# Summing the rotated state's two parts before the output products, and making four low-part weight tiles by accumulating transfers

## The chip, the cores and the metric

The kernel runs on one core of one Trainium2 chip. The metric is the device time of one execution in microseconds. Three runs of the kernel before are shown, and one further execution was profiled.

## What is computed

Two residual layers on a 256 x 1024 sequence, all in float32. The first mixes with a diagonal complex state-space model (S5) and a gated unit, the second with causal attention over one block of 256 keys. Cut to the part that the change touches:

```python
proj = h @ w_in; u, z = proj[..., :1024], proj[..., 1024:]
bu = einsum(u, b)                       # per group of 16 channels, 64 complex states
s_re, s_im = associative_scan(a, f * bu)
y = einsum(s_re, c_re) - einsum(s_im, c_im) + d_skip * u
y = gelu(y)
y = y * sigmoid(y @ w_glu + b_glu)      # the gated unit
y = y * silu(z)
h = h + y @ w_out
```

## The kernel before

**Who sets the order.** The body does not issue instructions: it records operations in a list (`Program.add`), each with a cost in ns that a formula gives, its dependencies and a push (a bonus in priority). `Program.order` lays them out with these costs in a list schedule, forth and back several times, and `emit` then issues them in the order of the planned starts. Each engine runs its own queue strictly in that order. So a changed cost, one operation more or a moved call changes the order on all five engines.

**Tiles.** The 64 groups of channels stand as four blocks b = 0 to 3. `x_table`, `x_turn`, `k_table`, `y_table` and `w_table` (L847 and above) build small matrices from the model's parameters. `u_step` (k = 0 to 7) makes u from x and eight 512 KB weight tiles, with the transposes `x_turn8` and `b_turn` in between, and behind them `c_turn` (L694): 16 transposes of c into a PSUM tile `wide`, which ScalarE copies to the tile `yT`. `u_turn` then scales u (by `rum`, which VectorE copies from PSUM as tile `s`), sends it through the transfers `zz<-zz` and transposes it into `U`. `z_pair` (m = 0 to 3) are 64 products of 128 x 256 for the gate z, whose operands are ready early. Each leaves two records in the trace, as all float32 products do (transposes leave one).

**States.** For each block, `ssm_in` (32 products of 64 x 64) brings u into the states, `rotate` turns them by cosines and sines (`EC`, `ES`, made by `rotations`) and scans them along time, and `states` (L886) turns the result back. That result has two parts, `pa` (tile `tb`) and `pc` (tile `t`): the state is their sum. It is never formed. `ssm_within` writes the block's own 16 products into PSUM, and `ssm_out` (L926) adds 32 products with `pa` and then 32 with `pc`, with the same other operand `Y`; PSUM does the sum. ScalarE copies the block out (`ys`), TensorE transposes it, ScalarE applies gelu into `yT` and a rounding copy into `ah`, and VectorE makes the low part `al`.

**Weights in two parts.** From weight tile 16 on, each 128 x 1024 tile w (loaded into `wr`, four buffers) becomes a high part (`X` or `zh`: a rounding copy on ScalarE) and a low part (`xp` or `zl`: w minus high on VectorE), in `split_part` (L474). Even tiles use `X` and `xp`, odd ones `zh` and `zl`. `mm3` makes three products of them. Tiles 16 to 23 belong to the gated unit (`glu_tile`, 24 products each, 192 in all), tiles 24 to 31 to the output product behind it.

```python
        act(hi, raw[i][:, c0:c1])
        tt(V, lo, raw[i][:, c0:c1], hi.bitcast(F), SUB)
```

All operations are issued in `emit`, so the trace has them all at L355, and tiles tell them apart.

Of the kernel before, what the change touches and what calls it, by code (L numbers as in the profile page):

```python
# [20 lines left out]
F = mybir.dt.float32  # L21
# [54 lines left out]
class Program:  # L76
# [67 lines left out]
    def add(self, handle, eng, method, a, k):  # L144
# [9 lines left out]
        if dma:  # L154
            cost = self.ISSUE[eng]
        elif eng == "PE":
            if method == "transpose":
                cost = 109 if aps[0].shape[0] >= 64 else 30
            else:
                m, c = n(aps[0]), n(aps[1])  # L160
                if aps[0].dtype == FR:
                    cost = 4 + 0.4455 * max(c, 256)
                else:
                    cost = max(4 * c / 2.4 + 2, 109) * m / 128 * aps[0].shape[0] / 128
                    if m == 32:
                        cost = 42
        elif eng == "DVE":
            two = method in ("tensor_tensor", "scalar_tensor_tensor", "tensor_tensor_scan", "tensor_reduce") or psum
            cost = (70 if not psum else 125) + n(aps[0] if method == "tensor_reduce" else out) * (6.4 if method == "reciprocal" else 2.1 if method == "tensor_tensor_scan" else 1.04 if two else 0.53)
        elif eng == "ACT":  # L170
            cost = 95 + 0.83 * n(aps[0]) + (60 if len(aps) > 1 else 0) + (100 if "accum_out" in k else 0)
        else:
            spread = any(not x.ap[-1][0] for x in aps)
            each = {"memset": 0.85, "tensor_scalar": 5.2}.get(method, 1.8 if spread else 2.2)
            cost = 150 + 205 * n(out) if k.get("op") == OP.pow else 60 + n(out) * each
# [25 lines left out]
        if eng == "ACT" and not dma:  # L201
            f = a[2] if len(a) > 2 else AF.Copy
            op.table = {AF.Silu: 0, AF.Sin: 0, AF.Gelu_apprx_tanh: 1, AF.Exp: 2}.get(f)
        if dma:
            run = out.ap[-1][1] if len(aps[0].ap) > 1 else 1
            run = min(aps[0].ap[-1][1], out.ap[-1][1]) if aps[0].ap[-1][0] == 1 else 1
            op.nbytes = int(np.prod(out.shape)) * 4 * (1 if run * 4 >= 512 else 2)
        for x, w in [(x, False) for x in aps] + [(x, True) for x in outs]:
# [19 lines left out]
                    keep.append(e)  # L228
            keep.append((op.i, w, p0, p1, bits))
            self.seen[name] = keep  # L230
    grouping, chain, only, behind, push = False, None, None, None, 0

    @contextmanager
    def fixed(self, only=None):
# [121 lines left out]


RATE = 270
MODE = 3000
TICK, BUSY = 10240 / 3, 3600  # L360
SAME = {"PE": 0, "DVE": 127, "ACT": 140, "POOL": 95, "SP": 0}
# [23 lines left out]
def body(ctx: ExitStack, tc: tile.TileContext, x, norm_g, w_in1, a_re, a_im, log_dt, b_re, b_im,  # L385
# [88 lines left out]
    def split_part(i, c0, c1):  # L474
        if i not in whl:
            load_to(i + 1)
            own = i % 2
            whl[i] = (tile_([128, 1024], FR, name="zh" if own else "X", bufs=NZ if own else NX),
                      tile_([128, 1024], FR, name="zl" if own else "xp", bufs=NZ if own else NP_))
        hi, lo = (w[:, c0:c1] for w in whl[i])  # L480
        act(hi, raw[i][:, c0:c1])
        tt(V, lo, raw[i][:, c0:c1], hi.bitcast(F), SUB)

    def split_to(n):
        while state["split"] < min(n, len(plan)):
# [96 lines left out]
    vec = tile_([128, 24], F, name="vec")  # L582
    PE.transpose(pt[:, 256:272], vn, ident[:16, :16])
    V.tensor_copy(vec[:, 0:16], pt[:, 256:272])
    xT = tile_([128, 8, S], F, name="ah")

    def x_turn8(k):
# [228 lines left out]
    def k_table(b):  # L816

        p = wide()
        xv = X[b].rearrange("p (r q x) -> p r q x", r=2, q=8)
        with prog.group():  # L820
            for r in range(2):
                for a in range(2):
                    for hh in range(4):
                        for j2 in range(2):
                            o = 512 * j2 + 16 * hh
                            PE.matmul(p[side(a), o:o + 16], xv[side(j2), r, 2 * hh + a], ct_[side(j2), r, 8 * b + 2 * hh + a],
                                      start=(r == 0 and hh == 0), stop=(r == 1), skip_group_check=True)
        kv = lambda t: t[:, 8 * b:8 * b + 8].rearrange("p (h j) c -> p h j c", j=2)
        tt(V, kv(KS), p.rearrange("p (j x) -> p j x", j=2)[:, :, 0:64].rearrange("p j (h c) -> p h j c", c=16), kv(dm), ADD)

# [16 lines left out]
    def ssm_in(b):  # L847

        p = wide()
        prog.push = 10000  # L850
        with prog.group():
            for ri in range(2):
                for hh in range(4):
                    for j2 in range(2):
                        for a in range(2):
                            o = 512 * a + (4 * ri + hh) * 64
                            PE.matmul(p[side(j2), o:o + 64], XT[b][side(a), 4 * ri + hh, side(j2)],
                                      U[side(a), 4 * b + hh, side(j2)], start=True, stop=True)
        prog.push = 0
        vts[b] = p  # L860

    PSTS = {}
# [23 lines left out]
    def states(b, t2, p):  # L886

        ec, es = (t[:, :, :M - 1] for t in turns[b])
        pa, pc = tmp("tb", NT), tmp("t3", NQ)
        gm = lambda t: t.rearrange("p (r g m) -> p r g m", r=2, m=M)  # L890
        first = lambda t: t.rearrange("p (g m) -> p g m", m=M)[:, :, 0]
        G.memset(first(pc), 0.0)
        ts(V, first(pa), p[1][:, 0:16], 0.0, 0.0, MIN, MAX)
        z = gm(t2)[:, :, :, :M - 1]
        tt(V, gm(pa)[:, :, :, 1:], z, bc(ec[:, None], [128, 2, 8, M - 1]), MUL)
        stt(V, gm(pc)[:, 0, :, 1:], z[:, 1], -1.0, es, MUL, MUL)
        tt(V, gm(pc)[:, 1, :, 1:], z[:, 0], es, MUL)
# [12 lines left out]
    def ssm_within(b):  # L910

        if b % 2:
            p = wide().rearrange("p (j x) -> p j x", j=2)
            p = p[:, 0], p[:, 1]
        else:
            p = acc(), acc()
        prog.push = 20000
        with prog.group():
            for h in range(4):
                for j2 in range(2):  # L920
                    for a in range(2):
                        product(p, h, a, j2, U[side(a), 4 * b + h, side(j2)], W[side(a), 8 * b + 2 * h + j2], h == 0, False)
        prog.push = 0
        return p

    def ssm_out(b, p):  # L926
        for i, t in enumerate(PSTS[b]):
            tv = t.rearrange("p (r a h m) -> p r a h m", r=2, a=2, h=4)
            with prog.group():
                for r in range(2):  # L930
                    for h in range(4):
                        for a in range(2):
                            for j2 in range(2):
# [29 lines left out]
    with prog.fixed("PE"):  # L963
        for k in range(8):
# [2 lines left out]
                x_turn8(n)  # L967
            if k == 1:
                b_turn()
    load_to(14)  # L970
    prog.push = 10000
    c_turn()
    prog.push = 0
    pv0 = wide()
    PE.transpose(pv0[:, 0:8], vb, ident[32:40, 32:40])
    V.tensor_copy(vec[:, 16:24], pv0[:, 0:8])
    for i in range(2):
        PE.matmul(pv0[:, 8:10], cst[:, C_RU + 128 * i:C_RU + 128 * i + 128], rse[:, i], start=(i == 0), stop=(i == 1))
    rum = small([128, 2])
# [342 lines left out]
```

## Time and profile before

| | us |
|---|---|
| three runs | 296.65, 296.05, 292.43 (median 296.05) |
| the profiled execution: its time | 293.73 |
| its span in the trace | 291.9 |
| outside the span | 1.8 |

The span is cut as follows: to 28 us loads, parameters and the first half of u; to 53 us the rest of u and the tables; to 109 us gate, states and their products; to 134 us the gated unit; then the output product, and from 150 us on attention. Times of rows are us from the span's start; TensorE has an engine for products (PE) and one for loading their weights (PEld).

### The profile page before, as it was taken

How to read it: one execution, taken by the hardware profiler on the slowest of the kernel's cores; microseconds unless marked ns; L12 is line 12 of the kernel's file. 1: busy time of each engine (PE TensorE's matmuls, PEld its weight loads, DVE VectorE, ACT ScalarE, POOL GpSimd, SP SyncE). 2: the span in 40 equal slices, each digit the busy share in tenths (PEclk: the TensorE clock that was granted, in tenths of full speed). 3: DMA queues.
4: the chain of work that ended last, by engine and by line, in shares of the span. 5: the costliest groups of instructions: out<-in, count | busy, mean ns of one | idle time of the engine just before them, and what ended most of it. 6: DMA issues, size and time to landing. Idle time of an engine off the chain costs nothing.

```text
span 291.9 us, 6324 instructions
## 1 busy us (share of the span) xinstructions
PE 280.2 (96%) x2551; PEld 229.0 (78%) x2551; DVE 214.9 (74%) x430; ACT 159.1 (55%) x306; POOL 22.7 (8%) x26
## 2 busy tenths in 40 slices
PE   8998999999998969999999999899999999999995
PEld 7454458888677859998888888678888799998884
DVE  0959789998958647976439648898679988699603
ACT  2579347377440358766429347557565766585300
POOL 3100013000000000000000014500013100000000
PEclk9999999999999988999999999999999999999999
DMA  5999454882000193876745643565245472434003
GB/s 177 244 331 277 126 161 122 213 227 76 0 2 2 39 271 131 240 216 207 212 137 153 209 149 138 165 201 187 96 138 162 136 214 77 144 120 166 6 0 144
DMA packets 41596, 43.91 MB, mean 150 GB/s; under 512 B 4552, under 2 KB 31136, under 8 KB 41504
## 3 DMA queue, kind: packets, MB, share of 16 engines
q1 hardware_dynamic: 40608, 42.68, 50.2%
q10 hardware_dynamic: 864, 0.82, 0.8%
q8 instruction: 20, 0.33, 0.5%
q14 instruction: 8, 0.07, 0.1%
q0 software_dynamic: 96, 0.02, 0.0%
HBM read 41.41 MB, written 1.05 MB: 145 GB/s over the span
## 4 chain that ended last, share of the span: by engine, by line
PE 73%; DVE 7%; DMA 6%; ACT 5%; issue 4%; POOL 3%; SPq 1%; ACTq 0%; POOLq 0%
PE uz L355 33%; PE acc L355 23%; PE wide L355 17%; DMA zz<-in_x_dram 4%; POOL sm L355 3%; DVE sm L355 2%; DMA wr<-in_attn_w_in_dram 2%; DVE D L355 2%; ACT ES L355 1%; SPq L355 1%; DVE xp L355 1%; DVE zl L355 1%; ACT EC L355 1%; DVE X L355 1%; ACT X L355 1%
## 5 line engine op out<-in xcount | busy, mean ns | idle before, releaser
L355 DVE TENSOR_TENSOR xp<-wr,X 128x1024 fp32r<-128x1024 f32 x28 | 34.0, 1222 | 13.8 <-ACT X L355 13.7
L355 DVE TENSOR_TENSOR zl<-wr,zh 128x1024 fp32r<-128x1024 f32 x28 | 34.1, 1219 | 6.6 <-ACT zh L355 6.5
L355 ACT ACTIVATE zh<-wr 128x1024 fp32r<-128x1024 f32 x28 | 29.4, 1056 | 15.7 <-PE uz L355 7.9
L355 ACT ACTIVATE X<-wr 128x1024 fp32r<-128x1024 f32 x28 | 29.5, 1057 | 14.7 <-PE uz L355 8.1
L355 PE MATMUL uz<-al,zh 128*128 128x256 f32 x96 | 24.5, 349 | 0.0
L355 PEld LDWEIGHTS uz<-al,zh 128*128 128x128 f32 x96 | 17.9, 190 | 2.7 <-issue 0.8
L355 POOL TENSOR_TENSOR sm<-sm,mhalf 128x4 f32<-128x4 f32 x8 | 13.7, 1714 | 50.7 <-DVE sm L355 50.6
L355 PE MATMUL uz<-zh,ah 128*128 128x512 f32 x40 | 17.6, 490 | 0.0
L355 PE MATMUL acc<-zh,ah 128*128 128x512 f32 x40 | 17.6, 484 | 0.0
L355 PE MATMUL uz<-zl,ah 128*128 128x512 f32 x40 | 17.1, 478 | 0.0
L355 PE MATMUL acc<-zl,ah 128*128 128x512 f32 x40 | 17.1, 476 | 0.0
L355 PE MATMUL uz<-al,zl 128*128 128x256 f32 x64 | 16.6, 389 | 0.0
L355 PEld LDWEIGHTS uz<-al,zl 128*128 128x128 f32 x64 | 11.4, 190 | 3.0 <-issue 1.6
L355 DVE TENSOR_TENSOR Y<-acc,Y 128x512 f32<-128x512 f32 x4 | 2.8, 691 | 11.4 <-PE acc L355 11.4
L355 PEld LDWEIGHTS acc<-zl,ah 128*128 128x128 f32 x40 | 7.5, 189 | 4.2 <-issue 3.3
L355 DVE TENSOR_TENSOR tb<-s,yT 128x512 f32<-128x512 f32 x16 | 10.7, 682 | 0.0
L355 ACT ACTIVATE ys<-acc 128x256 f32<-128x256 f32 (+1 forms) x8 | 3.8, 496 | 12.4 <-PE acc L355 12.3
L355 PEld LDWEIGHTS acc<-zh,ah 128*128 128x128 f32 x40 | 7.4, 190 | 3.9 <-issue 2.9
L355 PEld LDWEIGHTS uz<-zl,ah 128*128 128x128 f32 x40 | 7.3, 189 | 3.3 <-issue 2.2
L355 PEld LDWEIGHTS uz<-zh,ah 128*128 128x128 f32 x40 | 7.3, 189 | 3.3 <-issue 2.4
L355 PE MATMUL uz<-X,ah 128*128 128x512 f32 x24 | 9.9, 411 | 0.0
L355 PE MATMUL acc<-X,ah 128*128 128x512 f32 x24 | 9.8, 408 | 0.0
(279 smaller groups left out, 804.8 us busy)
## 6 DMA issues: line engine op xcount, KB each, us to landing
wr<-in_attn_w_in_dram SPq DMA_DIRECT2D x32, 512.0 KB, 4.2
zl<-in_ssm_w_in_dram SPq DMA_DIRECT2D x8, 512.0 KB, 6.8
wr<-in_ssm_w_glu_dram SPq DMA_DIRECT2D x8, 512.0 KB, 6.3
wr<-in_ssm_w_out_dram SPq DMA_DIRECT2D x8, 512.0 KB, 4.3
wr<-in_attn_w_out_dram SPq DMA_DIRECT2D x8, 512.0 KB, 4.3
zh<-in_ssm_w_in_dram SPq DMA_DIRECT2D x7, 512.0 KB, 8.4
zz<-zz SPq DMA_DIRECT2D x8, 128.0 KB, 2.3
Y<-in_x_dram SPq DMA_DIRECT2D x2, 512.0 KB, 5.2
```

The lines of the kernel that those rows point to most:

```text
L355: getattr(handle, method)(*map(self.real, a), **{q: self.real(v) for q, v in k.items()})
```

## The change

Five things are changed. (1) `SUM`: for all four blocks VectorE adds `pc` to `pa`, and `ssm_out` makes one set of 32 products instead of two. (2) `LOW_DMA`: for tiles 16 to 19 the low part isn't made on VectorE. ScalarE copies the negative high part into it, and GpSimd issues a transfer that adds the weight tile from DRAM on top (2 MB are thus read a second time). (3) `CT`: `c_turn` stands behind `u_step(5)` in the fixed order of TensorE, and not after `u_step(7)` with a push. (4) The transpose of `b_glu` and its copy into `vec` go to the start. (5) The planner's costs of small products are set one by one (`unit`).

```diff
-                    if m == 32:
-                        cost = 42
+                    if self.unit:
+                        cost = self.unit
...
+        if dma and "accum_op" in k:
+            op.nbytes = int(np.prod(out.shape)) * 8
...
+EARLY = {}
+CT = 5
+LOW_DMA = (16, 17, 18, 19)
+SUM = (0, 1, 2, 3)
...
         act(hi, raw[i][:, c0:c1])
-        tt(V, lo, raw[i][:, c0:c1], hi.bitcast(F), SUB)
+        if i in LOW_DMA:
+            act(lo, hi.bitcast(F), AF.Copy, scale=-1.0)
+            G.dma_start(lo.rearrange("p (k n) -> p k n", k=8), plan[i], accum_op=ADD)
+        else:
+            tt(V, lo, raw[i][:, c0:c1], hi.bitcast(F), SUB)
...
+    PE.transpose(pt[:, 272:280], vb, ident[32:40, 32:40])
+    V.tensor_copy(vec[:, 16:24], pt[:, 272:280])
...
         tt(V, gm(pc)[:, 1, :, 1:], z[:, 0], es, MUL)
+        if b in SUM:
+            tt(V, pa, pa, pc, ADD)
+            pc = None
         PSTS[b] = pa, pc
...
-        for i, t in enumerate(PSTS[b]):
-            tv = t.rearrange("p (r a h m) -> p r a h m", r=2, a=2, h=4)
+        parts_ = [t.rearrange("p (r a h m) -> p r a h m", r=2, a=2, h=4) for t in PSTS[b] if t is not None]
+        prog.unit = 31
+        for tv in parts_:
...
             if k == 1:
                 b_turn()
+            if k == CT:
+                c_turn()
...
-    prog.push = 10000
-    c_turn()
-    prog.push = 0
+    if CT > 7:
+        prog.push = 10000
+        c_turn()
+        prog.push = 0
     pv0 = wide()
-    PE.transpose(pv0[:, 0:8], vb, ident[32:40, 32:40])
-    V.tensor_copy(vec[:, 16:24], pv0[:, 0:8])
```

The three places below are all on ScalarE. In the names, the last number tells tiles of one name apart, the one before it the buffer.

The first place is before the scaling of u. `yT<-wide` is the copy of c, `EC` and `ES` are the cosines and sines of a block (1 or 2), `zz<-uz` is the scaled u. Before:

```order
L355 ACTIVATE ah_0_127<-wide_1_322,vec_0_120 128x256
L355 ACTIVATE ah_0_127<-wide_0_328,vec_0_120 128x256
L355 ACTIVATE D0_1_316<-D0_1_316 128x8
L355 ACTIVATE yT_0_267<-wide_1_341 128x512 x2
L355 ACTIVATE EC_2_378<-ES_2_259 128x512
L355 ACTIVATE EC_2_378<-EC_2_378,s13_0_93 128x512
L355 ACTIVATE ES_2_259<-ES_2_259 128x512
L355 ACTIVATE rrow_0_397<-wide_1_388 128x256
L355 ACTIVATE zz_0_410<-uz_0_138,s15_0_406 128x512
```

After:

```order
L357 ACTIVATE EC_1_357<-ES_1_201 128x512
L357 ACTIVATE EC_2_363<-ES_2_256 128x512
L357 ACTIVATE EC_1_357<-EC_1_357,s13_0_93 128x512
L357 ACTIVATE EC_2_363<-EC_2_363,s13_0_93 128x512
L357 ACTIVATE ES_1_201<-ES_1_201 128x512
L357 ACTIVATE yT_0_271<-wide_1_359 128x512 x2
L357 ACTIVATE ES_2_256<-ES_2_256 128x512
L357 ACTIVATE rrow_0_405<-wide_1_397 128x256
L357 ACTIVATE zz_0_414<-uz_0_137,s15_0_409 128x512
```

Block 1's three operations, which stood further up, now stand ahead of the copy of c, with two of block 2.

The second place is the second half of u. `um` is what comes back from the transfers, `U2<-acc` are the transposed tiles that `ssm_in` of blocks 2 and 3 reads, `X`, `xp` and `zh` belong to weight tiles 16 to 18. Before:

```order
L355 ACTIVATE um_0_639<-zz_0_410 128x8x64 x2
L355 ACTIVATE X_2_661<-wr_0_623 128x1024
L355 ACTIVATE zh_2_674<-wr_1_627 128x1024
L355 ACTIVATE U2_0_520<-acc_0_668 128x512
L355 ACTIVATE U2_0_520<-acc_1_671 128x512
```

After:

```order
L357 ACTIVATE um_0_604<-zz_0_414 128x8x64 x2
L357 ACTIVATE X_2_684<-wr_0_572 128x1024
L357 ACTIVATE xp_0_690<-X_2_684 128x1024
L357 ACTIVATE X_0_701<-wr_2_583 128x1024
L357 ACTIVATE U2_0_563<-acc_0_695 128x512
L357 ACTIVATE U2_0_563<-acc_1_697 128x512
```

Between `um` and `U2` stand three whole-tile copies instead of two: the high and the negative copy of tile 16, and the high part of tile 18.

The third place is the end of the states. `ys` are blocks copied out, `zz<-uz` the last two gate pairs, then gelu into `yT`. Before:

```order
L355 ACTIVATE ys_0_1117<-acc_0_966 128x16x16
L355 ACTIVATE ys_0_1117<-acc_1_969 128x16x16
L355 ACTIVATE ys_1_1176<-wide_0_984 128x16x16 x2
L355 ACTIVATE zz_0_793<-uz_0_913 128x2x4x64
L355 ACTIVATE zz_0_793<-uz_1_922 128x2x4x64
L355 ACT_TABLE_LOAD
L355 ACTIVATE yT_0_1284<-uz_0_1244 128x4x64
L355 ACTIVATE ys_0_1356<-acc_0_1156 128x16x16
L355 ACTIVATE ys_0_1356<-acc_1_1159 128x16x16
L355 ACTIVATE yT_0_1284<-uz_0_1244 128x4x64
```

After:

```order
L357 ACTIVATE ys_0_1111<-acc_0_982 128x16x16
L357 ACTIVATE ys_0_1111<-acc_1_985 128x16x16
L357 ACTIVATE ys_1_1117<-wide_0_1003 128x16x16 x2
L357 ACTIVATE zz_0_931<-uz_0_941 128x2x4x64
L357 ACTIVATE zl_0_1169<-zh_0_979 128x1024
L357 ACTIVATE zz_0_931<-uz_1_949 128x2x4x64
L357 ACT_TABLE_LOAD
L357 ACTIVATE yT_0_1216<-uz_0_1175 128x4x64 x2
L357 ACTIVATE ys_0_1267<-acc_0_1120 128x16x16
L357 ACTIVATE ys_0_1267<-acc_1_1123 128x16x16
```

The negative copy of tile 19 (`zl`) now stands between the last two gate pairs.

## Rows read from the trace of the kernel before

**Rows 1.** Page, part 1: busy time, share of the span and instructions.

```profile
PE 280.2 (96%) x2551; PEld 229.0 (78%) x2551; DVE 214.9 (74%) x430; ACT 159.1 (55%) x306; POOL 22.7 (8%) x26
```

**Rows 2.** Windows: us busy (instructions) of PE, PEld, DVE, ACT, POOL; clock, DMA share, GB/s.

```profile
108.00:112.00 4.00, 4.00 (x22) 3.66 (x21) 0.36 (x2) 3.17 (x9) 0.00 (x0) 0.62 0.88 296
112.00:133.00 21.00, 21.00 (x179) 21.00 (x178) 17.51 (x33) 14.66 (x28) 0.00 (x0) 1.00 0.63 185
```

**Rows 3.** Timeline, TensorE, first and last product of the gated unit.

```profile
109.30 0.56 PE L355 MATMUL wide<-ah,zh 128*128 128x256 f32 x1
...
133.54 0.28 PE L355 MATMUL wide<-ah,zl 128*128 128x256 f32 x1
```

**Rows 4.** Timeline, TensorE, 92 to 108 us (start, us, engine, operation, count [idle before]).

```profile
92.32 1.11 PE L355 MATMUL wide<-Y,tb 64*64 64x64 f32 x64
93.26 0.39 PE L355 MATMUL wide<-Y,t 64*64 64x64 f32 x11
94.59 0.98 PE L355 MATMUL wide<-Y,t 64*64 64x64 f32 x51 [0.94 <-issue]
...
99.56 1.56 PE L355 MATMUL uz<-al,zl 128*128 128x256 f32 x6
...
103.41 1.10 PE L355 MATMUL wide<-Y,t 64*64 64x64 f32 x61
107.42 0.33 PE L355 MATMUL wide<-Y,t 64*64 64x64 f32 x3 [2.92 <-issue]
```

**Rows 5.** Timeline, ScalarE, 101 to 115 us.

```profile
101.16 1.15 ACT L355 ACTIVATE zz<-uz 128x512 f32<-128x512 f32 x1 [2.39 <-PE uz L355]
102.33 1.28 ACT L355 ACT_TABLE_LOAD   x1
...
108.83 1.54 ACT L355 ACTIVATE yT<-uz 128x256 f32<-128x256 f32 x3 [3.05 <-PE uz L355]
110.17 0.69 ACT L355 ACTIVATE ys<-wide 128x256 f32<-128x256 f32 x2
110.75 0.64 ACT L355 ACTIVATE yT<-uz 128x256 f32<-128x256 f32 x1
...
114.51 0.43 ACT L355 ACTIVATE ah<-yT 128x256 fp32r<-128x256 f32 x1
```

**Rows 6.** Timeline, TensorE, 28 to 48 us.

```profile
28.15 1.21 PE L355 MATMUL wide<-cst,Y 64*128 64x64 f32 x16 [1.00 <-ACT ah L355]
...
47.33 1.09 PE L355 MATMUL uz<-cst,um 128*128 128x128 f32 x8 [0.22 <-ACT um L355]
```

**Rows 7.** Timeline, ScalarE, 29 to 41 us.

```profile
29.39 1.09 ACT L355 ACTIVATE yT<-wide 128x512 f32<-128x512 f32 x2 [0.82 <-PE wide L355]
34.85 0.63 ACT L355 ACTIVATE EC<-ES 128x512 f32<-128x512 f32 x1 [4.38 <-DVE ES L355]
...
40.00 0.69 ACT L355 ACTIVATE zz<-uz,s 128x512 f32<-128x512 f32 x1 [1.78 <-PE uz L355]
```

**Rows 8.** Timeline, VectorE, 34 to 40 us.

```profile
34.14 0.68 DVE L355 SCALAR_TENSOR_TENSOR ES<-ys,ES 128x512 f32<-128x512 f32 x1
...
39.62 0.15 DVE L355 COPY s<-wide 128x2 f32<-128x2 f32 x1
```

**Rows 9.** Timeline, ScalarE, 58 to 63 us.

```profile
58.20 1.06 ACT L355 ACTIVATE X<-wr 128x1024 fp32r<-128x1024 f32 x1 [0.28 <-DMA wr<-in_ssm_w_glu_dram]
...
61.94 1.09 ACT L355 ACTIVATE U<-acc 128x512 f32<-128x512 f32 x2 [0.57 <-PE acc L355]
```

**Rows 10.** Page, part 5: a whole-tile difference on VectorE (mean ns of one: 1219).

```profile
L355 DVE TENSOR_TENSOR zl<-wr,zh 128x1024 fp32r<-128x1024 f32 x28 | 34.1, 1219 | 6.6 <-ACT zh L355 6.5
```

**Rows 11.** Timeline, VectorE: the last step of the last state.

```profile
98.75 0.19 DVE L355 TENSOR_SCALAR tb<-wide 128x16 f32<-128x16 f32 x1 [0.79 <-PE wide L355]
```

**Rows 12.** Page, part 6: loads of the gated unit (KB each, median us to landing).

```profile
wr<-in_ssm_w_glu_dram SPq DMA_DIRECT2D x8, 512.0 KB, 6.3
```

**Rows 13.** Timeline, GpSimd: a transfer of 64 rows that it issues.

```profile
2.97 0.55 POOL L355 DMA_DIRECT2D s<-in_ssm_d_dram  x1 [0.20 <-POOL t L355]
```

More of the change, by code (lines that the diff above doesn't have):

```diff
@@ L203, in add @@
             op.table = {AF.Silu: 0, AF.Sin: 0, AF.Gelu_apprx_tanh: 1, AF.Exp: 2}.get(f)
-        if dma:
+        if dma and "accum_op" in k:
+            op.nbytes = int(np.prod(out.shape)) * 8
+        elif dma:
             run = out.ap[-1][1] if len(aps[0].ap) > 1 else 1
@@ L230, in add @@
             self.seen[name] = keep
-    grouping, chain, only, behind, push = False, None, None, None, 0
+    grouping, chain, only, behind, push, unit = False, None, None, None, 0, 0
     @contextmanager
@@ L480, in split_part @@
         hi, lo = (w[:, c0:c1] for w in whl[i])
+        prog.push = EARLY.get(i, 0)
         act(hi, raw[i][:, c0:c1])
-        tt(V, lo, raw[i][:, c0:c1], hi.bitcast(F), SUB)
+        if i in LOW_DMA:
[4 more added lines that the diff above has]
+        prog.push = 0
     def split_to(n):
@@ L819, in k_table @@
         xv = X[b].rearrange("p (r q x) -> p r q x", r=2, q=8)
+        prog.unit = 41
         with prog.group():
@@ L827, in k_table @@
                                       start=(r == 0 and hh == 0), stop=(r == 1), skip_group_check=True)
+        prog.unit = 0
         kv = lambda t: t[:, 8 * b:8 * b + 8].rearrange("p (h j) c -> p h j c", j=2)
@@ L849, in ssm_in @@
         p = wide()
-        prog.push = 10000
+        prog.push, prog.unit = 10000, 31
         with prog.group():
@@ L858, in ssm_in @@
                                       U[side(a), 4 * b + hh, side(j2)], start=True, stop=True)
-        prog.push = 0
+        prog.push = prog.unit = 0
         vts[b] = p
@@ L916, in ssm_within @@
             p = acc(), acc()
-        prog.push = 20000
+        prog.push, prog.unit = 20000, 66
         with prog.group():
@@ L922, in ssm_within @@
                         product(p, h, a, j2, U[side(a), 4 * b + h, side(j2)], W[side(a), 8 * b + 2 * h + j2], h == 0, False)
-        prog.push = 0
+        prog.push = prog.unit = 0
         return p
     def ssm_out(b, p):
-        for i, t in enumerate(PSTS[b]):
-            tv = t.rearrange("p (r a h m) -> p r a h m", r=2, a=2, h=4)
+        parts_ = [t.rearrange("p (r a h m) -> p r a h m", r=2, a=2, h=4) for t in PSTS[b] if t is not None]
+        prog.unit = 31
+        for tv in parts_:
             with prog.group():
@@ L934, in ssm_out @@
                                 product(p, h, a, j2, tv[side(j2), r, a, h],
-                                        Y[side(j2), r, 8 * b + 2 * h + a].rearrange("p k c -> p (k c)"), False, i == 1 and r == 1)
+                                        Y[side(j2), r, 8 * b + 2 * h + a].rearrange("p k c -> p (k c)"), False,
+                                        tv is parts_[-1] and r == 1)
+        prog.unit = 0
         ys = tile_([128, 4, 8, 16], F, name="ys", bufs=2)
@@ L969, in body @@
                 b_turn()
+            if k == CT:
+                c_turn()
     load_to(14)
-    prog.push = 10000
-    c_turn()
-    prog.push = 0
+    if CT > 7:
+        prog.push = 10000
+        c_turn()
+        prog.push = 0
     pv0 = wide()
-    PE.transpose(pv0[:, 0:8], vb, ident[32:40, 32:40])
-    V.tensor_copy(vec[:, 16:24], pv0[:, 0:8])
     for i in range(2):
```

## Prediction

> **What bounds the kernel now.** I read the busy shares first: TensorE is busy for 280.2 of 291.9 us [rows 1], so time goes only where its work goes, or one of its few gaps. Then the windows: in the gated unit it has 179 products in 21.00 us, 0.117 us each, with no gap and at full clock [rows 2]. The unit's last product starts at 133.54 [rows 3]. Behind it the order of every engine is the same in both kernels, up to tile names, so I forecast one number: by how much the end of the gated unit, at 133.65, moves.
>
> Then the timeline of TensorE ahead of it. From 51 us on it is full, with gate products (`uz<-al`) as filler; they end at 99.56 + 1.4 = 100.96 [rows 4]. There are two gaps, 0.94 us at 93.65 and 2.92 us at 104.5, both in the middle of a set of small products and both put down to "issue" [rows 4]. From the start of the 51 records behind the first gap to the end of the 61 before the second there are 384 records. With their weight loads that is 768 instructions, 3 x 256. I read these gaps as instruction fetch that came late, where 256 instructions take only some 2 us. The Trainium skill (Runtime: NRT & Kernel Launch, "Instruction fetch mechanics") has engines refill in blocks of 256 instructions, and holds that the refill is hidden. The spacing agrees with the block; the two gaps, 3.86 us together, don't agree with "hidden". By the rule alone nothing would be left to save there.
>
> Last the ScalarE timeline. From the table load at 102.33 a chain runs through gelu, block copies and rounding copies up to the last `ah` at 114.94 [rows 5]. The gated unit can't finish a tile without it.
>
> **The change part by part.** All in the time of the profiled execution.
>
> *The u turn.* `c_turn` behind `u_step(5)` takes away the gap of 1.00 us at 28.15 [rows 6], where it waited for its PSUM tile. But nothing follows early. ScalarE's copy of c, at 29.39 now [rows 7], stands behind two pairs of cosines and sines. VectorE makes the second of their inputs where it now starts the last one, so it is there at 34.15 [rows 8]; before, the same release gave `EC` at 34.85, a whole operation later [rows 7]. From 34.28: one more `EC` of 0.52, two sines of 0.62, one `ES` of 0.52, the two copies of c at 0.55 each: 37.66. VectorE's next six products of `Y` read c, and `rum` is copied behind them: 37.8 + 5 x 0.6 + 0.15 = 40.95 instead of 39.77 [rows 8]. ScalarE scales u at 41.1 instead of 40.00 [rows 7]. The transfers, `um` and TensorE's transposes at 47.33 [rows 6] hang on that: **+1.05 us** after 51 us. Bounds: -1.0 (the gap is saved, nothing is late) and +2.
>
> *Products.* A set of 32 takes 93.26 - 92.32 = 0.94 us [rows 4]. Four sets go, 3.8 us; against the point at which the gate products end, two `pc` sets go and one `pa` set is moved behind it: **-2.85 us**.
>
> *First fetch gap.* At 256 instructions apart, the edges now fall in sets that have gate products ahead of them: **-0.94**. A second edge falls three records before the end of the last set, and the block ahead of it holds the last two sets. I expect a late fetch there again, 1 to 3 us (before, the two blocks came about 3 and 5 us behind the edge ahead of them, which lies 128 records, some 2 us, ahead of each gap). ScalarE doesn't need that block for 5 us, so I cost it at nothing; were it needed at once, it would cost those 1 to 3 us.
>
> *The second half of u.* `um` comes 0.9 us earlier, as the far copies now precede `U`. But `U` then stands behind three whole-tile copies. The first waits for its load, at 58.20 now [rows 9] and about 57.3 then; three of 1.0 us with a hand-over end at 60.4. `U` starts there (61.94 before [rows 9]), `ssm_in` at 61.2. By my count of TensorE's list (ten gate products at 0.45, one `ssm_in`, one `k_table`, 16 transposes from 51.15) it gets there at 60.45: **+0.75**. Bounds 0 and 2.6.
>
> *Gate slots.* TensorE may not begin the third and fourth gate pair before ScalarE has evacuated the first two. ScalarE now has more ahead of these: **+0.9** (0.15 and 0.75), bounds 0 and 2.
>
> Together the gate products end at 100.96 + 1.05 - 2.85 - 0.94 + 0.75 + 0.9 = 99.9.
>
> *Tail on ScalarE.* The third pair's last product is three gate products earlier, 98.55. An evacuation takes 102.33 - 101.16 = 1.17 us [rows 5]: 98.75 to 99.9. The new negative copy takes 0.95, to 100.85. The fourth pair ends at 102.0, the table load (1.28) at 103.3. Gelu takes (110.17 - 108.83)/3 = 0.45, a pair of block copies 110.75 - 110.17 = 0.58 [rows 5], `ah` 0.31. Eight, two pairs and eight of them: 3.6 + 1.2 + 2.5 = 7.3, so the last `ah` ends at about 110.6 (114.94 before). Before, the second fetch gap stood in this chain; now nothing does.
>
> *Gated unit.* The last `al` follows 0.6 us later (half of a whole-tile operation [rows 10]). By then TensorE has made 30 of the 192 products: 10 groups of three need nothing later. It goes on at 111.4 (0.2 for hand-overs): 111.4 + 162 x 0.117 = 130.4. At 108 to 112 the granted clock was 0.62 (full speed before and after, so part of it at 1.2 GHz), after the gap of 2.92 us [rows 2, 4]. The same will follow the idle time before 110: I add 0.5, bounds 0 and 1.8. End 130.95, against 133.65: **-2.7 us**.
>
> *What costs nothing.* The four sums: VectorE, 1.22 us each [rows 10], where four low parts of the same 1.22 go. The last state ended at 98.94 [rows 11]; with all four on top, 103.8, its products end at 104.8, still ahead of ScalarE's need at 107. The transpose of `b_glu`: 0.2 us of an engine that waits for loads there. The negative copies: ScalarE, 4 x 1.0 us; two are counted above, the others lie in its idle time. The earlier loads of tiles 20 to 23: the 2 MB behind the second gap go, and the output product's loads take their place.
>
> *The accumulating transfers.* No row shows one. From below: a plain load of that size lands in 6.3 us [rows 12]. From above: GpSimd takes 0.55 us to issue 64 rows [rows 13]; a tile has 1024 pieces, 16 times that, 8.8 us, and reading and writing the target may double the 6.3 to 12.6, so 21.4. I take 8 us, nearest to the plain load. The last one (tile 19) is issued at about 100.1 and first read at the unit's 63rd product, 111.4 + 33 x 0.117 = 115.3, less what goes early, 114.4: 14.3 us. At 8 it is hidden; at 21.4 TensorE waits 7.1 us. Tile 17 has 23 us, tiles 16 and 18 more. The Trainium skill (DMA: Bandwidth & Descriptors, "Anatomy of one DMA — SWDGE (gpsimd) path") fits a plain transfer issued by GpSimd with 2.0 us plus bytes / 436e3, an estimated 3.2 us here; no run here shows it. By it the transfers are hidden with more to spare.
>
> **Sum.** The profiled execution, 293.73 with 1.8 outside its span, gives 291.0. The runs' median is 296.05, their lowest 292.43. I take the middle of profile and median, 294.9, as the level: **292.2 us**, with 287.5 to 296 as this case's own range from the bounds of the waits.
>
> **Rivals.** *No new wait* (faster). If `rum`, `U` and the gate slots come in time, all removed work shows: 3.8 + 1.0 + 3.86 = 8.7 us, 286.2. For it: TensorE is the bound at 96%. Against it: the three waits follow from the order on ScalarE, which TensorE can't pass. *Late accumulation* (slower). If a transfer of tile 19 takes over 14.3 us, each us more goes into the gated unit, from 17.0 us on the kernel is slower than before, and at 21.4 it loses 7.1 - 2.7 = 4.4: 299.3. With a clock that falls in that wait, as at 108 us, some 1 to 2 more. For it: nothing shows such a transfer, and on its queue it stands behind two clears. Against: the plain loads. *Nothing comes of it*: the tail on ScalarE is later than I have it (fetch at the last set, the gate slots' wait at 2 us), and the table load, which in my sum starts only 0.3 us earlier than at 102.33, comes 3 us later: 294.9.
>
> **How the numbers follow.** Forecast 0.55, no new wait 0.22, nothing 0.14, late accumulation 0.09. The range of 286.5 to 297.5 holds the forecast, nothing and the upper half of the first rival. Two per cent, about what a measurement here tells from no change, are 5.9 us. Faster by more: the first rival and a little of the forecast's lower end, 0.24. Slower by more: part of late accumulation, 0.06. The rest, 0.70, is within.
>
> **What would show it.** Right: the scaling of u at about 41; `ssm_in` of block 2 waiting for `U` at about 61; 128 fewer small products, no gap at 93; the last `ah` near 110.6; the unit's end near 131, with the same length after it. Wrong: TensorE waiting for a GpSimd transfer inside the unit, VectorE as the releaser of the products, or an end of the gate products away from 99.9 by over 2 us.

## The result and the profile after

The changed kernel is slower. Twenty runs of each on one chip: 297.97 us median (295.35 to 301.49) against 293.84 (290.34 to 296.65), a ratio of 1.0165 with a 95% interval of 1.0141 to 1.0188. The forecast was 292.2, its range ended at 297.5. The profiled execution is the shortest of the twenty: 295.35 us, with a span of 293.6 against 291.9. Here and below a median takes in all runs of a kernel, while a ratio leaves out those over 1.5% above its fastest.

The page first: parts 1, 3 (packets, MB, share) and 6 (us to landing) of the changed kernel's profile.

```profile
PE 279.4 (95%) x2295; PEld 226.5 (77%) x2295; DVE 215.1 (73%) x430; ACT 161.7 (55%) x310; POOL 29.9 (10%) x30
...
q8 instruction: 18, 0.29, 0.4%
...
xp<-in_ssm_w_glu_dram POOLq DMA_DIRECT2D x2, 512.0 KB, 8.2
```

TensorE lost 256 records (128 products), and yet is busy for only 0.8 us less than in [rows 1]: what remains runs slower in places. The accumulating transfers of tiles 16 and 18 land in 8.2 us in the median, and 8 were taken; one by one the four took 10.0, 6.2, 6.4 and 11.7 us, tiles 16 to 19. The slowest, tile 19's, in the DMA view of 95 to 130 us:

```profile
zl<-in_ssm_w_glu_dram POOLq DMA_DIRECT2D x1, 512.0 KB, 11.7
```

TensorE's timeline, to be held against [rows 3, 4, 6].

```profile
46.76 1.09 PE L357 MATMUL uz<-cst,um 128*128 128x128 f32 x8
49.22 2.42 PE L357 MATMUL wide<-yT,X 64*64 64x16 f32 x64 [1.37 <-DVE Y L357]
...
63.73 1.16 PE L357 MATMUL wide<-yT,X 64*64 64x16 f32 x56
67.92 0.41 PE L357 MATMUL wide<-yT,X 64*64 64x16 f32 x8 [3.03 <-issue]
...
71.09 1.81 PE L357 MATMUL acc<-Y,cst 64*64 64x512 f32 x4
...
98.36 1.16 PE L357 MATMUL acc<-Y,tb 64*64 64x64 f32 x64
99.34 1.11 PE L357 MATMUL wide<-Y,tb 64*64 64x64 f32 x64
...
103.02 2.86 PE L357 MATMUL uz<-al,zl 128*128 128x256 f32 x12
...
110.56 0.66 PE L357 MATMUL uz<-cst,ys 128*128 128x128 f32 x4 [1.49 <-ACT ys L357]
110.97 0.36 PE L357 MATMUL wide<-ah,zh 128*128 128x256 f32 x1
...
135.47 0.28 PE L357 MATMUL wide<-ah,zl 128*128 128x256 f32 x1
```

Both fetch gaps of [rows 4] are gone, and the sets that are left take 0.98 us each. But up to 47 us nothing was lost (the transposes at 46.76, 0.57 earlier than in [rows 6]), and then there are a wait of 1.37 us for VectorE, where the kernel before had 0.32, and a fetch gap of 3.03 us, where it had none. The gate products end at 105.8, not 100.96; the gated unit's last product starts at 135.47, 1.93 later than in [rows 3]. The windows show the rest (us, busy of PE, PEld, DVE, ACT, POOL; clock, DMA share, GB/s).

```profile
47.00:51.00 4.00, 2.63 (x64) 2.40 (x64) 3.05 (x7) 2.74 (x5) 1.84 (x1) 0.72 0.51 124
51.00:55.00 4.00, 4.00 (x28) 3.39 (x25) 3.84 (x7) 0.00 (x0) 0.00 (x0) 0.50 0.94 257
...
65.00:70.00 5.00, 2.08 (x36) 1.66 (x40) 1.71 (x4) 1.93 (x4) 0.00 (x0) 0.93 0.98 140
70.00:75.00 5.00, 5.00 (x66) 3.27 (x59) 5.00 (x6) 2.40 (x7) 0.00 (x0) 0.73 0.35 105
```

In these windows (a clock of 1 is 2.4 GHz) the granted clock is down with each of the two stalls: 0.72 and 0.50 from 47 to 55 us, 0.73 from 70 to 75. From 51 to 55 TensorE is never idle, and works at 1.2 GHz throughout. The four W records (`acc<-Y,cst`) at 71.09 take 1.81 us where a kernel at full clock (a2 below) needs 1.04.

ScalarE and VectorE, against [rows 5, 7, 8].

```profile
39.73 1.27 ACT L357 ACTIVATE zz<-uz,s 128x512 f32<-128x512 f32 x2 [2.49 <-DVE s L357]
...
107.66 1.28 ACT L357 ACT_TABLE_LOAD   x1
...
115.43 0.78 ACT L357 ACTIVATE ah<-yT 128x256 fp32r<-128x256 f32 x2
```

```profile
35.86 0.69 DVE L357 TENSOR_TENSOR Y<-s,yT 128x512 f32<-128x512 f32 x1 [2.92 <-ACT yT L357]
...
39.48 0.15 DVE L357 COPY s<-wide 128x2 f32<-128x2 f32 x1
...
45.43 2.49 DVE L357 TENSOR_TENSOR Y<-s,yT 128x512 f32<-128x512 f32 x4
48.87 0.29 DVE L357 TENSOR_TENSOR Y<-wide,Y 128x128 f32<-128x128 f32 x1 [0.95 <-POOL Y L357]
```

The copy of `rum` and the scaling of u come when they came before, not 1.1 us later. VectorE's first skip sum (48.87) reads the skip products out of the PSUM tile `wide` that TensorE needs next, and the skip table, a tile that GpSimd makes; it waits 0.95 us for that table. ScalarE's tail begins 5.3 us later than in [rows 5] and ends 1.3 later, at 116.2.

### The profile page after: what moved, and what is told of

Same layout as the page of the kernel before. It is cut to its first block, busy times and chain, and to the rows that moved or that the text cites. A ratio compares the mean times of both kernels' runs of the same rounds, so it can differ in the third digit from the quotient of the medians.

```text
span 293.6 us, 5827 instructions
## 1 busy us (share of the span) xinstructions
PE 279.4 (95%) x2295; PEld 226.5 (77%) x2295; DVE 215.1 (73%) x430; ACT 161.7 (55%) x310; POOL 29.9 (10%) x30
## 3 DMA queue, kind: packets, MB, share of 16 engines
HBM read 43.51 MB, written 1.05 MB: 152 GB/s over the span
## 4 chain that ended last, share of the span: by engine, by line
PE 66%; DVE 12%; ACT 6%; POOL 6%; issue 4%; DMA 4%; SPq 1%; ACTq 0%; DVEq 0%; POOLq 0%
PE uz L357 31%; PE acc L357 20%; PE wide L357 15%; POOL sm L357 4%; DMA zz<-in_x_dram 4%; DVE X L357 2%; DVE sm L357 2%; DVE tb L357 2%; POOL Y L357 2%; DVE D L357 1%; ACT zz L357 1%; ACT EC L357 1%; SPq L357 1%; DVE Y L357 1%; DVE xp L357 1%
## 5 line engine op out<-in xcount | busy, mean ns | idle before, releaser
L357 DVE TENSOR_TENSOR xp<-wr,X 128x1024 fp32r<-128x1024 f32 x26 | 31.7, 1221 | 14.4 <-ACT X L357 14.1
L357 DVE TENSOR_TENSOR zl<-wr,zh 128x1024 fp32r<-128x1024 f32 x26 | 31.7, 1218 | 6.3 <-ACT zh L357 6.3
L357 PE MATMUL uz<-al,zh 128*128 128x256 f32 x96 | 27.2, 368 | 0.3 <-ACT zz L357 0.3
L357 PE MATMUL uz<-al,zl 128*128 128x256 f32 x64 | 15.7, 386 | 0.0
L357 PE MATMUL wide<-yT,X 64*64 64x16 f32 x256 | 6.8, 223 | 4.4 <-issue 3.0
L357 DVE TENSOR_TENSOR tb<-s,yT 128x512 f32<-128x512 f32 x16 | 10.7, 682 | 0.0
L357 PEld LDWEIGHTS wide<-yT,X 64*64 64x64 f32 x256 | 6.4, 155 | 4.9 <-issue 3.3
```

What stands on the lines that cost most here:

```text
L357: getattr(handle, method)(*map(self.real, a), **{q: self.real(v) for q, v in k.items()})
```

## The experiments

Three theories. **A**: the u turn's new place makes the skip table late, TensorE waits 1.37 us, and that opens the slow clock. **B**: the loads of tiles 20 and 22 and the accumulating transfer of tile 16, which now fall at 60 us, hold up TensorE's instruction fetch. (The expectations below call tile 22 tile 21, and tile 18's transfer tile 17's; by the kernel's order of loads and splits they are 22 and 18.) **C**: the tail on ScalarE and VectorE before the gated unit sets the time. In a1 to a3, b2 to b4, c1 and c2 every engine's order is written out as the planner gave it to the changed kernel, in c4, d1 and d3 as it gave it to a4, in d2 as to b1, so that one move is one move; a4, b1 and c3 are ordered anew:

```diff
-        for o in self.order():
+        for o in (self.ops[i] for i in PIN):
```

All times are medians; ratios, with their 95% intervals, are to the kernel before on the same chip.

**a1, the skip table sooner.** Places in the order written out:

```diff
 PE   wide<-cst,X x8
+PE   wide<-cst,s x4
 PE   acc<-zl,ah x4
 PE   wide<-cst,X x8
-PE   wide<-cst,s x4
 ACT  xp<-wide
+ACT  s<-wide
 ACT  xp<-wide
-ACT  s<-wide
```

> The changed kernel with every engine's order written out as it ran, and one thing moved: the two small products of the skip table, their copy on ScalarE and the table on GpSimd come one turn of X earlier, so that GpSimd can start some 2 us sooner. Theory A (the u turn's move made the table late): TensorE's wait of 1.37 us at 49.22 goes to under 0.3, the granted clock from 47 to 55 us comes back from 0.5-0.7 to 1.0, and the time falls by 2 to 3.5 us, to about 295. Theory B (the fetch gap of 3.03 us at 64.89 with its slow clock is the loss): the wait goes but the gap stays, and at most 1.4 us are gained, 296.6 or more. Theory C (the tail on ScalarE and VectorE before the gated unit sets the time): nothing, 298.

297.86 us, 1.0156 [1.0106, 1.0206]: nothing gained. The wait stayed, and here is why: GpSimd's table in the changed kernel, in a1 and in a4, one row each.

```profile
44.28 4.56 POOL L357 TENSOR_TENSOR Y<-s,cst 128x512 f32<-128x512 f32 x1 [25.68 <-ACT s L357]
```

```profile
44.07 6.76 POOL L357 TENSOR_TENSOR Y<-s,cst 128x512 f32<-128x512 f32 x1 [23.48 <-ACT s L357]
```

```profile
45.98 1.06 POOL L357 TENSOR_TENSOR Y<-s,cst 128x512 f32<-128x512 f32 x1 [26.08 <-ACT s L357]
```

And VectorE in a1:

```profile
47.43 2.48 DVE L357 TENSOR_TENSOR Y<-s,yT 128x512 f32<-128x512 f32 x4
50.87 0.29 DVE L357 TENSOR_TENSOR Y<-wide,Y 128x128 f32<-128x128 f32 x1 [0.95 <-POOL Y L357]
```

The table takes 1.06 us where VectorE is idle (a4). In a1 it was begun earlier against VectorE's work and took 2.2 us more: it ends at 50.83, 0.92 after VectorE's run of two-input instructions ends at 49.91, and in the changed kernel 0.92 after that run too (47.92, 48.84). The Trainium skill (SBUF — State Buffer, "Who interferes with whom") has a VectorE instruction with two SBUF inputs and a GpSimd instruction that reads SBUF exclude each other for the whole instruction; these rows agree.

**a2, the traffic behind.** Same kernel; SyncE's, GpSimd's and ScalarE's order:

```diff
-SP   wr<-in_ssm_w_glu_dram (tile 20)
-SP   wr<-in_ssm_w_glu_dram (tile 22)
 SP   zh<-in_ssm_w_in_dram
+SP   wr<-in_ssm_w_glu_dram (tile 20)
+SP   wr<-in_ssm_w_glu_dram (tile 22)
-POOL xp<-in_ssm_w_glu_dram (tile 16)
 POOL xp<-in_ssm_w_glu_dram (tile 18)
+POOL xp<-in_ssm_w_glu_dram (tile 16)
-ACT  X<-wr (tile 20)
 ACT  zh<-wr (tile 17)
+ACT  X<-wr (tile 20)
```

> The changed kernel in its own order, but the loads of tiles 20 and 21 behind the z weight's load on SyncE's queue, the whole-tile copy of tile 20 two copies later on ScalarE, and the accumulating transfer of tile 16 behind that of tile 17 on GpSimd's, so that 1.5 MB leave the stretch from 60 to 69 us. Theory B (these transfers hold up TensorE's instruction fetch): the gap of 3.03 us at 64.89 falls under 0.6, the clock from 70 to 75 us comes back from 0.73 to 1.0, and the time falls by 3.5 to 4.7 us, to about 294. Rival B2 (the gap belongs to 256 instructions that pass in 7 us, whatever is transferred): it stays at 2.5 to 3 us, and the time at 297.5 to 298. Theory A: the time falls by nothing at this place. Theory C: 298, what is gained here is waited for at 110 us.

292.06 us, 0.9953 [0.9915, 0.9991]: 5.9 us below the changed kernel, and faster than before, from the places of three transfers and a copy. TensorE's order is untouched. Its gap behind the 56th of the 64 skip records is gone; one of 1.23 is left 128 records ahead of it, where the first loads are still under way. Timeline and windows of a2:

```profile
49.18 1.44 PE L357 MATMUL wide<-yT,X 64*64 64x16 f32 x64 [1.34 <-DVE Y L357]
...
59.87 0.60 PE L357 MATMUL acc<-cst,um 128*128 128x128 f32 x4 [1.23 <-issue]
...
65.80 1.04 PE L357 MATMUL acc<-Y,cst 64*64 64x512 f32 x4
```

```profile
47.00:51.00 4.00, 2.66 (x74) 2.27 (x73) 3.05 (x7) 2.74 (x5) 1.80 (x1) 1.00 0.48 116
51.00:55.00 4.00, 4.00 (x64) 3.28 (x66) 3.96 (x8) 2.29 (x4) 0.00 (x0) 1.00 0.93 260
...
65.00:70.00 5.00, 5.00 (x83) 3.83 (x80) 5.00 (x6) 3.09 (x10) 0.00 (x0) 1.00 0.75 208
70.00:75.00 5.00, 5.00 (x83) 3.57 (x82) 5.00 (x7) 3.97 (x6) 0.88 (x1) 1.00 0.79 215
```

The wait for the skip table is still there, 1.34 us, and yet the clock is 1.00 behind it: such a wait isn't followed by the slow clock in each execution. So of the 4.7 us between the two profiles some 3.1 (0.28 x 4 + 0.5 x 4, the clock of the changed kernel from 47 to 55 us) lie ahead of the transfers that were moved, which can't have caused them. What the move is worth is told by the medians; how its 5.9 us divide into fetch and clock isn't shown.

**a3, both moves.** 

> Both moves of the two runs before in one kernel. Theories A and B together: their gains add, 5.5 to 7.5 us below the changed kernel, about 291.5, faster than before by 0.8%. Theory B alone: 294. Theory C (ScalarE's and VectorE's tail before the gated unit): 296 or more, with TensorE's wait at 110 us grown from 1.49 to over 4 us.

292.79 us, 0.9985 [0.9946, 1.0024]: as a2; no fetch gap at all, but the wait near 50 us and a clock of 0.50 from 51 to 55. Theory C falls with a2 and a3: TensorE's wait at the tail stays at 1.49.

**b2 and b3, one kind of traffic each.** b2 moves only the two loads (and the copy of tile 20), b3 only the accumulating transfer.

> The changed kernel in its own order, with the loads of tiles 20 and 21 alone moved behind the z weight's (and the copy of tile 20 two places later); the accumulating transfer of tile 16 stays. If the loads on SyncE hold up the fetch: gap near 65 us under 1.3, time 292 to 293 as with both moved. If the accumulating transfer does: gap still 2.5 to 3.3 us, time 296 to 298. If both share it: about 295.

> The mirror of the run before: the accumulating transfer of tile 16 alone goes behind that of tile 17, the loads of tiles 20 and 21 stay at 60 us. If the accumulating transfer holds up the fetch: gap near 65 us under 1.3, time 292 to 293. If the loads do: gap 2.5 to 3.3 us and 296 to 298. If both share it: about 295.

295.89 us, 1.0097 [1.0065, 1.0129], with a gap of 1.94; and 294.68, 1.0035 [1.0000, 1.0070], with gaps of 1.91 and 0.56 at the two edges. Both share it.

**a4, the sums alone.**

```diff
-CT = 5
-LOW_DMA = (16, 17, 18, 19)
+CT = 8
+LOW_DMA = ()
```

> Only the summed states: the low parts of tiles 16 to 19 on VectorE and the u turn behind the steps as in the kernel before; the planner orders it anew. Theory B: no transfer but SyncE's early loads, no gap over 1 us from 57 to 72 us, and a time of 292 to 294.5 (the products' 3.8 us gained, some of it given to a fetch gap near 100 us). Theory A: the skip table is as late as in the changed kernel (the planner puts it at the same place), so a wait of 1 to 1.4 us near 49 and the slow clock stay: 295 to 296. Theory C (the sums on VectorE are the loss): 298 as the changed kernel.

289.79 us, 0.9875 [0.9827, 0.9923], better than any theory gave. Its profile has no wait near 50 us, one fetch gap (2.21) where before has two (3.86), and full clock: the sums alone gain 1.3%, and the moved turn and the accumulating transfers lose 2.9 points of the ratio. (Parts 4 and 5 of the change stay in a4; none of the runs takes them out.)

**c4 and d3, half of the loads later.** If B holds, a4's gap must shrink when its loads do:

```diff
-SP   wr<-in_ssm_w_glu_dram (tile 17)
-SP   wr<-in_ssm_w_glu_dram (tile 19)
 SP   zh<-in_ssm_w_in_dram
+SP   wr<-in_ssm_w_glu_dram (tile 17)
+SP   wr<-in_ssm_w_glu_dram (tile 19)
-ACT  zh<-wr (tile 17)
 ACT  BW<-acc x2
+ACT  zh<-wr (tile 17)
```

> The summed states alone (289.8 us) in their own order, with the loads of tiles 17 and 19 moved behind the z weight's, some 15 us later, and the copy of tile 17 behind the next two W copies on ScalarE; nothing on TensorE moves. Theory B: with 1 MB and not 2 in flight from 52 us on, the queues are empty before TensorE passes the fetch boundary at 60.4 us, the gap of 2.21 us at 62.59 falls under 0.8, and the time to 287.5 to 288.5. Rival B2 (the gap is a matter of the instructions alone): 2 us of gap stay, 289.8.

> The kernel of c4 once more, as the base of d1 on the same chip and for a narrower interval. If its 288.2 us stand: 287.5 to 289, a ratio to before of 0.98 to 0.985, no wait near 50 us and a clock of 1.0 from 47 to 60 us. If c4's four runs were luck: 289.5 to 290.5, as the summed states with all loads early.

288.19 us, 0.9829 [0.9763, 0.9896], and 288.40, 0.9816 [0.9769, 0.9864]: the fastest version of the study, 1.8% below before. TensorE at the same edge, and the window ahead of it, in a4:

```profile
62.59 1.10 PE L357 MATMUL wide<-U,xp 64*64 64x64 f32 x59 [2.21 <-issue]
```

```profile
55.00:60.00 5.00, 5.00 (x210) 4.59 (x208) 4.68 (x9) 3.80 (x6) 0.00 (x0) 1.00 0.99 267
```

and in c4:

```profile
61.64 1.10 PE L357 MATMUL wide<-U,xp 64*64 64x64 f32 x59 [0.69 <-issue]
```

```profile
55.00:60.00 5.00, 5.00 (x198) 4.59 (x196) 4.68 (x8) 2.94 (x6) 0.00 (x0) 1.00 0.66 171
```

The DMA share falls from 0.99 to 0.66 and the gap from 2.21 to 0.69; in d3's profile no gap is left. Theory B stands by these gaps and by a2; the times alone don't part a4 from c4 and d3, whose intervals overlap. Nor is traffic the whole of it: the gap of 0.94 us before [rows 4] came with empty queues. From 88 to 95 us of before one packet moved, the instruction block itself:

```profile
DMA packets 1, 0.02 MB, mean 2 GB/s; under 512 B 0, under 2 KB 0, under 8 KB 0
```

Small products alone can outrun the fetch by that much; traffic makes the gap longer.

**b4, c1 and c2, the wait for the skip table.** b4 lets VectorE make the table, last of its run. c1 also moves the sum that reads it ahead:

```diff
-    tt(G, dm, bc(dk[:, :, None], [128, 32, 16]), bc(cst[:, C_I16:C_I16 + 16][:, None, :], [128, 32, 16]), MUL)
+    tt(V, dm, bc(dk[:, :, None], [128, 32, 16]), bc(cst[:, C_I16:C_I16 + 16][:, None, :], [128, 32, 16]), MUL)
 DVE  Y<-s,yT x2
+DVE  Y<-s,cst
+DVE  Y<-wide,Y
 DVE  Y<-s,yT x2
-DVE  Y<-wide,Y
```

c2 is c1 with the moves of a2.

> The changed kernel in its own order, with the skip table made by VectorE (0.68 us, last of the run of table instructions before the first sum that reads it) and not by GpSimd, whose end came 0.92 to 0.95 us after the end of VectorE's run whenever it began. Theory A2 (VectorE's run holds GpSimd off, and the wait opens the slow clock): TensorE's wait of 1.37 us at 49.22 falls to 0.9 to 1.1, the gap at 65 us stays; time 297 to 298 if the clock is unchanged, 295 if the slow clock from 47 to 60 us hangs on the longer wait.

> The changed kernel in its own order, but the skip table on VectorE, and with the first sum that reads it moved ahead of the last two of the table instructions, so that the bank is free before TensorE asks for it. Theory A2 (the wait of 1.37 us at 49.22 opens the slow clock that follows in most runs until 60 us): the wait is under 0.4, the granted clock from 47 to 60 us is 1.0, the fetch gap near 65 us stays, and the time is 294 to 295.5. Rival A3 (the slow clock comes by itself, or from the small products): clock 0.5 to 0.8 from 51 to 55 as before, time 297 to 298.

> The edit of the run before, and the loads of tiles 20 and 21 and the accumulating transfer of tile 16 moved behind as in a2. All parts of the change are kept, only their places differ. Theories A2 and B together: no gap over 1.3 us on TensorE from 28 to 110 us but ScalarE's at 42 to 44 and 104, clock 1.0 to 105 us, time 288.5 to 290.5. Rival A3: as a2, 292.

b4: 298.18 us, 1.0181 [1.0133, 1.0229]; the wait is 1.12, nothing gained. c1: 296.16, 1.0110 [1.0056, 1.0165]; the wait is gone, but 0.76 is waited for a table a little later, the clock is 0.70 from 51 to 55, and the fetch gap of that profile is the largest seen:

```profile
69.51 0.55 PE L357 MATMUL wide<-yT,X 64*64 64x16 f32 x8 [4.40 <-issue]
```

c2: 291.94, 0.9936 [0.9903, 0.9969]: no more than a2, as the rival A3 had it, though its profile has a clock of 1.00 throughout. Theory A's gains don't come in any of the three.

**d1, the wait put in.** The other way round, in c4's kernel, which had no wait there:

```diff
-DVE  Y<-wide,Y
 DVE  X<-s,yT x2
 DVE  X<-X,tb x2
+DVE  Y<-wide,Y
```

> The kernel of c4 (summed states, half of the loads later) with one thing moved: VectorE does the four instructions of the next X table ahead of the first skip sum, so that the bank comes free some 2.4 us later and TensorE waits 1.5 to 1.9 us near 50 us where it waited for nothing. Theory A2 (such a wait opens the slow clock): clock 0.5 to 0.7 somewhere from 51 to 60 us, a loss of 1.7 and 2 to 3 more, 291.5 to 293. Rival A3 (the slow clock has nothing to do with it): clock 1.0 there, at most 1.7 us lost, 288.2 to 290.

291.75 us, 0.9939 [0.9899, 0.9979], 3.35 above d3: twice the wait. d1's timeline and windows, then d3's windows:

```profile
51.68 1.44 PE L357 MATMUL wide<-yT,X 64*64 64x16 f32 x64 [1.66 <-DVE Y L357]
```

```profile
51.00:55.00 4.00, 3.32 (x72) 3.10 (x73) 2.37 (x6) 0.91 (x2) 0.00 (x0) 0.80 0.75 188
55.00:60.00 5.00, 5.00 (x152) 4.26 (x150) 3.06 (x7) 3.01 (x4) 0.00 (x0) 0.82 0.69 175
```

```profile
51.00:55.00 4.00, 4.00 (x82) 3.39 (x78) 4.00 (x8) 2.06 (x5) 0.00 (x0) 1.00 0.73 179
55.00:60.00 5.00, 5.00 (x204) 4.67 (x200) 4.92 (x9) 2.94 (x6) 0.00 (x0) 1.00 0.74 185
```

A wait of 1.66 us, and a clock of 0.80 and 0.82 over the 9 us behind it, worth 0.2 x 4 + 0.18 x 5 = 1.7 us. The other executions agree: over the whole span the ten of d1 have a mean clock of 0.980 to 0.993, the ten of c4 and d3 one of 0.992 to 1.000. So an added wait does bring more of the slow clock, at this place, but not each time (a2), and that one of this length is needed isn't shown: c1 had the slow clock with 0.76 us. The way back failed too: c2 turned a2's wait of 1.34 us into one of 0.77, and gained nothing.

**b1, c3 and d2, which part brings which loss.** b1 is the changed kernel with `LOW_DMA = ()`, c3 with `CT = 8`, both ordered anew; d2 is b1 in its own order with c1's edit.

> The changed kernel with the low parts of tiles 16 to 19 on VectorE again (no accumulating transfers), the u turn and the sums as changed; the planner orders it anew and lets one early load (tile 20) go instead of two. Theory B (the transfers of 60 to 69 us and the fetch): as the summed states alone, 289.5 to 291.5. Rival D (the u turn's move costs as much as it gives): 292 to 294, above the summed states alone by more than 2 us. Rival E (the whole-tile copies on ScalarE, which go too, were free): no other difference.

> The changed kernel with the u turn behind the steps as before; sums and accumulating transfers as changed, ordered anew by the planner (table on GpSimd 2.5 us earlier, loads of tiles 20 and 21 at the same early place, transfer of tile 16 as early). Theories A2 and B: no wait for the sum near 49 us and no slow clock there, but a fetch gap of 2 to 3.5 us between 58 and 70 us and a slow clock behind it; 293.5 to 295.5. Rival F (the turn's move is the loss, the transfers are not): 290 to 291, as the summed states alone.

> The kernel of b1 (summed states and the moved u turn, low parts on VectorE) in its own order, with the skip table on VectorE and the first skip sum right behind the products it reads, so that TensorE's wait of 1.96 us at 47.26 goes. Theory A2: the wait and the clock of 0.69 and 0.50 from 47 to 55 us go (1.96 and 3.2 us in that profile), 290 to 291.5. Rival A3: the wait goes and the clock stays: 293 to 294.5. Rival D (the turn's place costs by something else): 295.

b1: 295.42 us, 1.0026 [0.9984, 1.0069]. Against the sums alone the moved turn costs 1.5 points of the ratio, as rival D had it (over 2 us), though it put the time at 292 to 294; its profile shows a wait of 1.96 us for the skip sum, a clock of 0.69 and 0.50 from 47 to 55 us, and fetch gaps of 0.75 and 2.04. c3: 295.87, four runs of 292.29, 294.15, 297.60 and 298.13, too few and too far apart for an interval; its profile has no wait for the skip sum, full clock to 65, gaps of 0.94 and 2.48, and 0.66 from 65 to 70. Even the lowest of the four lies above all of a4's (288.71 to 290.35): the transfers lose much of the sums' gain without the turn. d2: 295.34, 0.9994 [0.9940, 1.0048]: the wait for the skip sum and the slow clock from 47 to 60 are gone from its profile (0.96 us is waited for an X table at 48.96), but the runs scatter from 290.9 to 298.0, and this profile is of one of the shorter, 291.99. What the turn's new place costs beside wait and clock stays open.

**All profiles together.** Take from each span the fetch gaps from 50 to 110 us and the share of it that the clock's mean withheld (an estimate: it charges idle time too).

| kernel | span | fetch gaps | clock | rest |
|---|---|---|---|---|
| before | 291.9 | 3.86 | 0.994 | 286.3 |
| after | 293.6 | 3.03 | 0.983 | 285.6 |
| a2 | 288.9 | 1.23 | 0.994 | 285.9 |
| a4 | 287.8 | 2.21 | 0.999 | 285.3 |
| b1 | 292.7 | 2.79 | 0.983 | 284.9 |
| b2 | 294.0 | 1.94 | 0.977 | 285.3 |
| b4 | 297.1 | 4.89 | 0.983 | 287.2 |
| c1 | 296.1 | 4.40 | 0.981 | 286.1 |
| d3 | 286.4 | 0.00 | 0.994 | 284.7 |

The spans differ by 10.7 us, the rest by 2.5 (284.0 to 287.5 with the kernels left out). Most of what tells these profiles apart is late instructions and a slow TensorE. Part of the rest is the execution and not the kernel: the nine kernels in the order of after are the same up to the two small transposes `wide<-cst,s`, and these start at 36.41 in after, at 36.38 in a2 and at 38.41 in a1, ahead of all that was moved. The runs say the same of the clock: the twenty of after have a mean of 0.982, those of before beside a1 0.994; by the same estimate 1.8% of 298 less 0.6% of 294, 3.6 us, nearly as much as the whole difference of 4.1. What the products save goes into gaps and waits.

## Why the prediction was wrong, step by step

**The products**: right in size, four sets of 0.98 us gone, and with them the gaps of [rows 4]. Alone they are worth 1.3% (a4). From before to after and a4 the rest column above falls by only 0.7 to 1.0 for them: new waits of TensorE take the difference, in after 0.38 and 0.88 us for ScalarE at 42 to 44, 1.37 for VectorE at 49.22 and 1.49 for ScalarE at 110.56.

**"What costs nothing ... The earlier loads of tiles 20 to 23"**: this is the main step that failed; the u turn below is the second. It put the loads at nothing because of what they leave (the place behind the second gap), and did not look at what they and the first accumulating transfer fall on: TensorE's densest stretch of small products, with a fetch edge at either end. Moving them away is worth 5.9 us (a2), the loads alone 2.1 (b2) and the transfer alone 3.3 (b3). The prediction had read the gaps of [rows 4] as late fetches, but asked only where the edges go, not what traffic the fetch has to pass. Those gaps did go, as the term of -0.94 and the text on the second one have it; 3.03 us came at an edge not looked at.

**The u turn, +1.05**: wrong in mechanism. VectorE reads c from 35.86 on, not from 37.8, and the copy of `rum` ends at 39.63, not at 40.95. What the new order does cost is seen at the skip table: made on GpSimd while VectorE is busy, it holds up the first skip sum, and TensorE behind it for 1.37 us. The step followed what comes late only as far as u. By b1 the turn costs 1.5 points of the ratio; what of it isn't this wait stays open (d2).

**The clock, +0.5 for the gated unit**: wrong place and size. From 108 to 112 and from 112 to 133 it is 1.00 this time; the loss lies at 47 to 55 and 70 to 75 us, and is there 0.28 x 4 + 0.5 x 4 + 0.27 x 5 = 4.5 us of the profiled execution (an estimate: it charges the end of the wait too). No term was put behind any new wait, since none was seen.

**Second half of u, +0.75, and gate slots, +0.9**: TensorE doesn't wait for `U` at all, and 0.35 us for the slot.

**Tail and gated unit**: the gate products end at 105.8 instead of 99.9, which the prediction had named as a sign of being wrong (over 2 us away), and the rest followed: the last `ah` at 116.2 (110.6 forecast), the unit's end 4.6 later than forecast, 1.9 later than before.

**Accumulating transfers**: 8 us were taken, the four took 6.2 to 11.7, and the last, on which the sum hung, 11.7 of the 14.3 that the forecast gave it. No product waited for one, so the rival of late accumulation didn't come, and that its 299.3 lies nearest to the measured 297.97 is chance; the transfers cost by their traffic, not by their landing. The rival "nothing comes of it" (294.9) had no loss, and its reasons, a late fetch at the last set and a gate slot's wait of 2 us, didn't occur; only the table load came late, by 5.3 us and not by 3.

**The level**: 294.9, from three runs and the profile, lay 1.1 above the median of twenty, 293.84. Against the kernel before, the forecast was -2.7 us and the result +4.1.

## What to carry to other kernels

Before a transfer is moved, look at what TensorE does at its new time: here a run of small products used up 256 instructions in some 2 us, and a block that came late under full DMA queues cost up to 4.4 us (c1), often with a slow clock behind it. A wait of 1.66 us put in among small products cost twice its length (d1), but shortening one from 1.34 to 0.77 us gave nothing back (c2), so measure what such a wait costs before a planner is given a price for it. When parts of a change are bundled, measure each alone: here one part was worth 1.3% and the other two took more than that away.

## What the runs showed of the hardware

**Instruction blocks can be seen.** The page of after has 18 instruction packets of 16 KB, before has 20. TensorE's records, weight loads counted, make 2 x 2295 = 4590 = 17.9 x 256, and 2 x 2551 = 19.9 x 256: by this count they are TensorE's. The Trainium skill (Runtime: NRT & Kernel Launch, "Instruction fetch mechanics") states this block; that its fetch is mostly hidden doesn't hold at the gaps shown here. The packet at the gap of 3.03 us, in the DMA view of 65.5 to 65.6 us of after:

```profile
q8 instruction: 1, 0.02, 54.9%
```

TensorE goes on at 67.92, 2.3 us after that packet began. For the gaps that end at 94.59 and 107.42 before, 62.59 in a4 and 59.87 in a2, the packet is found at 92.3, 104.7, 59.9 and 57.1: always 2.3 to 2.8 us ahead, with empty queues (92.3) as with full ones. So I read the gap as the fetch, and what makes it longer under traffic lies ahead of its packet; what that is, isn't shown.

**GpSimd's table** took from 1.06 to 6.76 us for the same instruction, by what VectorE did beside it. **An accumulating transfer** of 512 KB holds GpSimd for 1.6 us and landed in 6.2 to 11.7 us after its issue, in the changed kernel.
